# The running sum of a depthwise convolution moved from SBUF to a PSUM bank of its own

## The chip, the cores and the metric

One Trainium2 chip, one of its cores. The metric is the device time of one execution in microseconds (us); three runs of the kernel before gave 3067.32, 3067.44 and 3069.30 us, median 3067.44 us.

## The reference

Two decoder layers over 1024 tokens of width 1024, all in fp32. In each layer one projection `z = h @ w_in` feeds three things: differential attention (4 heads, two softmaxes each), a causal depthwise convolution with 31 taps over 512 channels, and the gates of the two branches.

```python
z = h @ w_in[l]                                   # q | k | v | conv input | gates
sc = where(mask, einsum('bhcqd,bhckd->bhcqk', qb, kt) * scale, neg)
p = softmax(sc); a = p[:, :, 0] - lam * p[:, :, 1]
o = rms_norm(einsum('bhqk,bhkv->bhqv', a, vt), subln_g[l])
u = ga * sigmoid(gb)
u = causal_depthwise_conv(u, dw_conv_w[l], dw_conv_b[l])      # 31 taps
y_conv = silu(layer_norm(u, conv_ln_g[l], conv_ln_b[l])) @ w_conv_o[l]
mixed = (sigmoid(gA) * (o @ w_attn_o[l]) + sigmoid(gC) * y_conv) @ w_out[l]
x = x + (1 + gate1) * mixed
x = x + (1 + gate2) * SwiGLU(rms_norm(x) * (1 + scale2) + shift2)
```

## The kernel before

Everything is held feature-major: 128 features on the partitions, 1024 tokens in two halves of 512 columns. Each fp32 operand of a matmul is split into a high and a low part, and three products (high x high, high x low, low x high) are summed in one PSUM bank, so a 128x512 output tile of the z projection is 24 matmuls. There are eight PSUM banks of 128x512 fp32, shared out to three pools: `pmain` (2 banks, `pmt`), `pscore` (3, `psct`) and `pone` (3, `p1`).

In a layer the z projection and the attention run mixed. PLAN names the order in which the parts are written: P is the projection of q, k, v of a head (tiles pq, pk, pv), A the attention of a head, g the gate projections (pg, 16 of them), C the convolution. A scheduler then fixes, before the run, the order of the instructions on each engine: it takes what is ready, by the order of writing, against a model of time. On the chip each engine runs its list strictly in order. While TensorE (PE) waits for the softmax of a block, what can stand between its attention matmuls is projection work (pk, pq, pv, pg); the text calls these the filler. There is a fixed stock of it in each layer.

The attention of a head goes in 8 blocks of 128 queries. A block has scores (psc), row maxima on VectorE (DVE), exponentials on ScalarE (ACT), the difference of the two softmaxes on DVE (L450), then for every 512 keys: up to four transposes into a bank `pat` of `pone`, a copy ath on ACT, a rest atl on DVE, and matmuls of both into a bank `po` of the same pool. po is held until DVE has read it (ov, L470). The next block needs its own po and pat. After four blocks, pot (again `pone`) turns the half head round.

The convolution comes in 8 pieces (channel group, half). Two of them run on ACT and GpSimd (POOL); the other six on DVE: one TENSOR_SCALAR for tap 0 (L607) and 30 SCALAR_TENSOR_TENSOR (L609) that read the input window `u` and the running sum `acc`, both in the SBUF tile uc, and write `acc`. That makes 180 instructions of L609 in a layer. They stand between the attention's DVE instructions wherever the scheduler saw DVE free.

At the start of layer 1, eight tiles pg of the projection (four slabs, two halves) grow together, a matmul each as the parts of h come. They use all eight banks.

Of the kernel before, what the change touches and what calls it, by code (L numbers as in the profile page):

```python
# [9 lines left out]
F32 = mybir.dt.float32  # L10
# [3 lines left out]
ALU = mybir.AluOpType  # L14
AX = mybir.AxisListType
PSUM = bass.MemoryType.PSUM
DRAM = bass.MemoryType.DRAM

P = 128
# [4 lines left out]
HF = 512  # L24
# [3 lines left out]
CONV_K = 31  # L28

CONV = ((0, 0, 0), (0, 1, 1), (1, 0, 0), (2, 0, 0), (3, 0, 0), (1, 1, 1), (2, 1, 0), (3, 1, 0))  # L30
SCB = 3
# [5 lines left out]
VB_CB = VB_CW + NCH * CONV_K  # L37
# [24 lines left out]
def trunk(tc, a):  # L62
    nc = tc.nc
    V, G, S, PE, DQ = nc.vector, nc.gpsimd, nc.scalar, nc.tensor, nc.sync
    top = ExitStack()
# [9 lines left out]
    dr = top.enter_context(tc.tile_pool(name="scratch", bufs=1, space=DRAM))  # L75
    pm = top.enter_context(tc.tile_pool(name="pmain", bufs=2, space=PSUM))
    psc = top.enter_context(tc.tile_pool(name="pscore", bufs=SCB, space=PSUM))
    p1p = top.enter_context(tc.tile_pool(name="pone", bufs=8 - 2 - SCB, space=PSUM))

    def p1(name, w=HF):  # L80
        return p1p.tile([P, w], F32, tag="p1", name=name)
# [1 line left out]
    def nt(name, w=HF, dt=F32):  # L83
        return ntp.tile([P, w], dt, tag="nt", name=name, bufs=4)

    def pmt(name):
        return pm.tile([P, HF], F32, tag="pm", name=name)

    def psct(name):
        return psc.tile([P, HF], F32, tag="sc", name=name, bufs=SCB)  # L90
# [31 lines left out]
    def vcol(l, base, j=0):  # L122
        o = l * VW + base + j
        return vec[:, o:o + 1]
# [4 lines left out]
    def wslab(src, nk, pl=None, nj=1):  # L129
        w = nk * nj * P  # L130
        raw = wp.tile([P, w], F32, tag="wraw", name="wraw", bufs=2)
        if nj > 1:
            DQ.dma_start(raw.rearrange("p (j k) -> p j k", j=nj), src.rearrange("j p k -> p j k"))
        else:
            DQ.dma_start(raw, src)
        wh, wl = ((pl or wp).tile([P, w], F32R, tag=n, name=n, bufs=2) for n in ("wh", "wl"))
        S.copy(wh, raw)  # L137
        G.tensor_tensor(wl, raw, wh.bitcast(F32), op=ALU.subtract)  # L138
        return wh, wl
# [150 lines left out]
    def sum_sq(Sq, xs, hf, j, E=None):  # L290

        hs = slice(hf * HF, hf * HF + HF)
        if j == 0:
            S.activation(Sq, xs[j][:, hs], AF.Square)
        else:
            t = nt("sqt")
            S.activation(t, xs[j][:, hs], AF.Square)
            (E or V).tensor_tensor(Sq, Sq, t, op=ALU.add)
# [17 lines left out]
    def rstd_bcast(Sq, inv_n, eps, name):  # L316

        return rstd_spread(rstd_diag(Sq, inv_n, eps, p1("pst"), 4, nt("dg")), p1(name), 4)
# [217 lines left out]
    for l in range(L):  # L536
# [27 lines left out]
        for hf in range(2):  # L564
            hs = slice(hf * HF, hf * HF + HF)
            for i in range(4):
                c = i // 2
# [19 lines left out]
        def conv(work):  # L587
            E = V
            for c, hf, on_pool in work:
                uc = cvp.tile([P, 2 * HF + CONV_K - 1], F32, tag="cv", name="uc", bufs=2)  # L590
                u, acc = uc[:, 0:HF + CONV_K - 1], uc[:, HF + CONV_K - 1:]
                if hf == 0:
                    G.memset(u[:, 0:CONV_K - 1], 0.0)
                    DQ.dma_start(u[:, CONV_K - 1:], ud[c][:, 0:HF])
                else:
                    DQ.dma_start(u, ud[c][:, HF - CONV_K + 1:T])
                for k in range(CONV_K):
                    w = vcol(l, VB_CW, c * CONV_K + k)
                    if on_pool:
                        if k == 0:  # L600
                            S.activation(acc, u[:, 0:HF], AF.Identity, bias=vcol(l, VB_CB, c), scale=w)
                        else:
                            t = A.tile([P, HF], F32, tag="ct", name="ct", bufs=1)
                            S.activation(t, u[:, k:k + HF], AF.Copy, scale=w)  # L604
                            G.tensor_tensor(acc, acc, t, op=ALU.add)  # L605
                    elif k == 0:
                        E.tensor_scalar(acc, u[:, 0:HF], w, vcol(l, VB_CB, c), op0=ALU.mult, op1=ALU.add)  # L607
                    else:
                        E.scalar_tensor_tensor(acc, u[:, k:k + HF], w, acc, op0=ALU.mult, op1=ALU.add)  # L609
                DQ.dma_start(cd[c][:, hf * HF:hf * HF + HF], acc)  # L610

        def conv_norm_steps():
# [183 lines left out]
        for hf in range(2):  # L796
            hs = HS[hf]
            Sq = nt("Sq")
            for j in range(KT):
                ps = psct("pwo")  # L800
                linear_half(ps, wslab(a["w_out"][l, j], KT), mrhs, KT, hf)
                if hf == 0:
                    DQ.dma_start(xs[j], xsrc[j])
                V.scalar_tensor_tensor(xs[j][:, hs], ps, gcol[l][0][:, j:j + 1], xs[j][:, hs],
                                       op0=ALU.mult, op1=ALU.add)
# [10 lines left out]
        for jj in range(4):  # L816
            a11, a12 = (xs[jj][:, h] for h in HS)
            a21, a22 = (xs[4 + jj][:, h] for h in HS)
            E = (V, G)[jj % 2]
# [107 lines left out]
                self.out(1, self.u4, self.c22)  # L927

        wtags = itertools.cycle(("wh", "wl"))
        banks = itertools.cycle((psct, p1, psct, p1, psct, p1, pmt, pmt))  # L930
        gs = [Group(f) for f in range(FT)]
        for g in gs[:2]:
            g.load()
# [22 lines left out]
        def gblock(hf, b):  # L956
            if b == NB - 1:
                u = hunit("gt", GP, "G", 9)
                un = [u[:, 0:2, :], u[:, 2:4, :]]
            else:  # L960
                un = [hunit(f"g{n}") if b >= 3 + hf else hunit(f"g{n}", GP, "G", 9) for n in "hl"]
            for k in range(4 * b, min(4 * b + 4, FT)):
                t = GP.tile([P, HF], F32, tag="gs", name="gs", bufs=5)
                DQ.dma_start(t, gf[k][:, HS[hf]])
                split_into(un[0][:, k % 4, :], un[1][:, k % 4, :], t, V if k % 2 else G)
            return un
# [9 lines left out]
        def ada_next(t):  # L976

            m2 = small("m2", 2)
            for h in range(2):
                raw = GP.tile([P, HF], F32, tag="gs", name="adraw", bufs=5)  # L980
                DQ.dma_start(raw, a["ada_w"][l + 1, t][:, HS[h]])
                V.scalar_tensor_tensor(raw, raw, 1.0, cs1[:, HS[h]], op0=ALU.mult, op1=ALU.mult,
                                       accum_out=m2[:, h:h + 1])
            m = modb[l + 1][:, t:t + 1]
            V.scalar_tensor_tensor(m, m2[:, 0:1], m2[:, 1:2], vcol(l + 1, t), op0=ALU.add, op1=ALU.add)
            ada_use(l + 1, t)
# [5 lines left out]
        for hf in range(2):  # L992
            hs = HS[hf]
            Sq = nt("Sq")
            for jq in range(2):
                js = range(4 * jq, 4 * jq + 4)
                pss = [(psct, psct, psct, pmt, pmt, p1, p1, p1)[j]("pfo") for j in js]
                last = hf and jq
                steps = [(b, q) for b in range(NB) for q in range(2)]
                if last:  # L1000
                    steps = [(b, q) for q in range(2) for b in reversed(range(NB))]
                seen = [0, 0]
                for b, q in steps:
                    k0, k1 = 4 * b, min(4 * b + 4, FT)
                    wh, wl = wslab(a["w_ffn_out"][l, js[2 * q]:js[2 * q] + 2, :, k0 * P:k1 * P], k1 - k0, nj=2)
                    bh, bl = gb[hf][b]
                    for jj in range(2):
                        ps = pss[2 * q + jj]
                        for k in range(k0, k1):
                            wc = slice((jj * (k1 - k0) + k - k0) * P, (jj * (k1 - k0) + k - k0 + 1) * P)  # L1010
                            PE.matmul(ps, wh[:, wc], bh[:, k % 4, :], start=(not seen[q] and k == k0), stop=False)  # L1011
                            PE.matmul(ps, wh[:, wc], bl[:, k % 4, :], start=False, stop=False)  # L1012
                            PE.matmul(ps, wl[:, wc], bh[:, k % 4, :], start=False,  # L1013
                                      stop=(seen[q] == NB - 1 and k == k1 - 1))
                    seen[q] += 1
                    for t in itertools.islice(ada_t, 3):
                        ada_next(t)
                    if hf == 0 and q == 1 and (b == 0 if jq == 0 else b < NB - 1):
                        gb[1].append(gblock(1, len(gb[1])))
                    if seen[q] == NB:  # L1020
                        for j in js[2 * q:2 * q + 2]:
                            V.scalar_tensor_tensor(xs[j][:, hs], pss[j % 4], g2[:, j:j + 1], xs[j][:, hs],  # L1022
                                                   op0=ALU.mult, op1=ALU.add)
                            sum_sq(Sq, xs, hf, j)
                            if l + 1 < L:
                                DQ.dma_start(xd[j][:, hs], xs[j][:, hs])
            pb = rstd_bcast(Sq, 1.0 / D, 1e-6, "prn")
            if l + 1 < L:
                hs_parts[hf] = norm_half(xs, hf, pb, acol[l + 1][0], modb[l + 1][:, 0:8], "h")
            else:  # L1030
                for j in range(KT):
                    y = nt("y")
                    V.scalar_tensor_tensor(y, xs[j][:, hs], vec[:, FG + j:FG + j + 1], pb,  # L1033
                                           op0=ALU.mult, op1=ALU.mult)
                    DQ.dma_start(a["out"][j][:, hs], y)
# [59 lines left out]
```

## Time and profile before

| | |
|---|---|
| median of 3 runs | 3067.44 us |
| the profiled execution | 3075.94 us, span 3074.0 us |
| busy: PE, DVE, POOL, ACT | 2800.3, 1980.2, 1779.4, 1154.6 us |
| mean granted TensorE clock | 0.964 of full speed |
| where L609 stands | 127 to 470 us (layer 1), about 1630 to 1945 us (layer 2) |

The profiled execution took 8.5 us more than the median. A row of instructions gives their busy time and the mean of one; a row of windows gives, for a stretch, how long each engine was busy in it. What PE was not busy in a stretch is what it waited there. [...]

### The profile page before, as it was taken

What the parts mean: (1) busy time and instruction counts of PE and PEld (TensorE: products, weight loads), DVE (VectorE), ACT (ScalarE), POOL (GpSimd) and SP (SyncE); (2) the same over time, 40 slices, a digit from 0 to 9 for tenths busy, and PEclk for the clock granted to TensorE, in tenths of its full rate; (3) what the DMA queues carried; (4) which work ended last, traced back from release to release, by engine and by line L of the source; (5) the groups of instructions that cost most, each with busy time, mean ns of one, the idle gap of its engine ahead of it and who ended that gap; (6) DMA issues with size and microseconds to landing.
All of it is one profiled execution on the core that took longest, in us unless ns stands there. A gap on an engine that the chain in (4) does not pass through costs nothing. (4 is left out here: it accounts for less than half of the span.)

```text
span 3074.0 us, 35430 instructions
## 1 busy us (share of the span) xinstructions
PE 2800.3 (91%) x12544; PEld 2285.4 (74%) x12544; DVE 1980.2 (64%) x2997; ACT 1154.6 (38%) x2059; POOL 1779.4 (58%) x1256
## 2 busy tenths in 40 slices
PE   4888889999979999889899888999998899998998
PEld 3666668887758888667788676788876688886786
DVE  8899997654565445578628999764546656664222
ACT  4235545443433333332322455544535233333321
POOL 6856674444676666554542686554356766666643
PEclk9989999999989999999999999999998899999999
DMA  7611111245322222388432111122552322225433
GB/s 271 223 56 66 56 59 52 83 154 203 123 103 90 83 83 83 106 264 288 155 116 89 45 53 58 66 76 84 177 192 76 123 79 84 85 83 174 138 117 93
DMA packets 151952, 353.92 MB, mean 115 GB/s; under 512 B 15328, under 2 KB 28000, under 8 KB 151776
## 3 DMA queue, kind: packets, MB, share of 16 engines
q1 hardware_dynamic: 151776, 351.67, 33.7%
q8 instruction: 99, 1.62, 0.2%
q14 instruction: 77, 0.63, 0.1%
HBM read 282.30 MB, written 69.30 MB: 114 GB/s over the span
## 5 line engine op out<-in xcount | busy, mean ns | idle before, releaser
L138 POOL TENSOR_TENSOR wl<-wraw,wh 128x1024 fp32r<-128x1024 f32 (+1 forms) x216 | 520.5, 2411 | 550.5 <-ACT wh L137 371.2
L609 DVE SCALAR_TENSOR_TENSOR uc<-uc,vec 128x512 f32<-128x512 f32 x360 | 386.7, 1074 | 5.8
L137 ACT CAST wh<-wraw 128x1024 fp32r<-128x1024 f32 (+1 forms) x216 | 219.5, 1017 | 433.3 <-PE pfo L1012 178.2
L778 POOL TENSOR_TENSOR wt<-wraw,wt 128x512 fp32r<-128x512 f32 x172 | 243.9, 1419 | 167.9 <-ACT wt L777 167.6
L1011 PE MATMUL pfo<-gh,wh 128*128 128x512 f32 x640 | 256.1, 402 | 31.1 <-ACT gh L777 22.0
L147 PE MATMUL pg<-hl,wh 128*128 128x512 f32 x640 | 253.7, 398 | 14.2 <-DVE hl L532 14.1
L146 PE MATMUL pg<-hh,wh 128*128 128x512 f32 x640 | 255.0, 403 | 11.8 <-ACT hh L531 8.9
L1013 PE MATMUL pfo<-gh,wl 128*128 128x512 f32 x640 | 243.4, 400 | 12.5 <-POOL wl L138 12.3
L1012 PE MATMUL pfo<-gl,wh 128*128 128x512 f32 x640 | 254.3, 397 | 0.0
L777 ACT CAST wt<-wraw 128x512 fp32r<-128x512 f32 x172 | 107.0, 622 | 322.7 <-PE pf L877 219.8
L605 POOL TENSOR_TENSOR uc<-uc,ct 128x512 f32<-128x512 f32 x120 | 163.6, 1363 | 66.2 <-ACT ct L604 65.4
L150 PE MATMUL pg<-hh,wl 128*128 128x512 f32 x640 | 172.6, 398 | 0.0
L439 ACT ACTIVATE e<-psc,nb 128x512 f32<-128x512 f32 (+2 forms) x192 | 110.1, 577 | 158.7 <-DVE nb L436 149.7
L1011 PEld LDWEIGHTS pfo<-gh,wh 128*128 128x128 f32 x640 | 123.8, 194 | 60.7 <-ACT gh L777 22.9
L1013 PEld LDWEIGHTS pfo<-gh,wl 128*128 128x128 f32 x640 | 123.0, 192 | 47.2 <-POOL wl L138 21.7
L147 PEld LDWEIGHTS pg<-hl,wh 128*128 128x128 f32 x640 | 121.5, 190 | 40.5 <-DVE hl L532 17.3
L1022 DVE SCALAR_TENSOR_TENSOR x<-pfo,gcol,x 128x512 f32<-128x512 f32 x32 | 23.7, 745 | 197.2 <-PE pfo L1013 196.7
L146 PEld LDWEIGHTS pg<-hh,wh 128*128 128x128 f32 x640 | 122.8, 192 | 36.3 <-ACT hh L531 9.4
L1012 PEld LDWEIGHTS pfo<-gl,wh 128*128 128x128 f32 x640 | 123.1, 192 | 25.9
L150 PEld LDWEIGHTS pg<-hh,wl 128*128 128x128 f32 x640 | 118.8, 190 | 23.4
L778 POOL TENSOR_TENSOR wt<-fraw,wt 128x512 fp32r<-128x512 f32 x88 | 118.7, 1349 | 21.1 <-ACT wt L777 21.1
L604 ACT ACTIVATE ct<-uc,vec 128x512 f32<-128x512 f32 x120 | 86.7, 722 | 113.9 <-POOL uc L605 113.0
(323 smaller groups left out, 7738.8 us busy)
## 6 DMA issues: line engine op xcount, KB each, us to landing
wraw<-in_w_ffn_out_dram SPq DMA_DIRECT2D x80, 512.0 KB
wraw<-in_w_in_dram SPq DMA_DIRECT2D x72, 512.0 KB
adraw<-in_ada_w_dram SPq DMA_DIRECT2D x48, 512.0 KB
adraw<-in_ada_w_dram SPq DMA_DIRECT2D x96, 256.0 KB
fraw<-in_w_ffn_in_dram SPq DMA_DIRECT2D x44, 512.0 KB
wraw<-in_w_ffn_in_dram SPq DMA_DIRECT2D x44, 512.0 KB
gs<-gf SPq DMA_DIRECT2D x88, 256.0 KB
gd<-graw SPq DMA_DIRECT2D x64, 256.0 KB
```

The source lines that it names most:

```text
L137: S.copy(wh, raw)
L138: G.tensor_tensor(wl, raw, wh.bitcast(F32), op=ALU.subtract)
L146: PE.matmul(ps, wh[:, wc], rhs(0, k, hf), start=(k == 0), stop=False)
L147: PE.matmul(ps, wh[:, wc], rhs(1, k, hf), start=False, stop=False)
L150: PE.matmul(ps, wl[:, wc], rhs(0, k, hf), start=False, stop=(k == nk - 1))
L439: S.activation(e[:, n0:n1], pss[b][:, 0:n1 - n0], AF.Exp, bias=nb, scale=0.125, accum_out=sx[:, 2 * b + c:2 * b + c + 1])
L605: G.tensor_tensor(acc, acc, t, op=ALU.add)
L609: E.scalar_tensor_tensor(acc, u[:, k:k + HF], w, acc, op0=ALU.mult, op1=ALU.add)
L778: E.tensor_tensor(lo, src, hi.bitcast(F32), op=ALU.subtract)
L1011: PE.matmul(ps, wh[:, wc], bh[:, k % 4, :], start=(not seen[q] and k == k0), stop=False)
L1012: PE.matmul(ps, wh[:, wc], bl[:, k % 4, :], start=False, stop=False)
L1013: PE.matmul(ps, wl[:, wc], bh[:, k % 4, :], start=False, stop=(seen[q] == NB - 1 and k == k1 - 1))
```

## The change

A fourth PSUM pool, `pconv`, has one bank (`pct`); `pone` has two banks instead of three. On DVE, taps 0 to 29 now write the running sum to that bank and read it from there; tap 30 reads it there and writes `acc` in SBUF, from where the transfer to DRAM goes as before. The two pieces on ACT and POOL are as they were. Two lists of banks in the feed-forward part take the new bank in the place of the third of `pone`.

```diff
-    p1p = top.enter_context(tc.tile_pool(name="pone", bufs=8 - 2 - SCB, space=PSUM))
+    p1p = top.enter_context(tc.tile_pool(name="pone", bufs=8 - 3 - SCB, space=PSUM))
+    pcv = top.enter_context(tc.tile_pool(name="pconv", bufs=1, space=PSUM))
...
+    def pct(name):
+        return pcv.tile([P, HF], F32, tag="pc", name=name)
...
                     elif k == 0:
-                        E.tensor_scalar(acc, u[:, 0:HF], w, vcol(l, VB_CB, c), op0=ALU.mult, op1=ALU.add)
+                        pc = pct("pc")
+                        E.tensor_scalar(pc, u[:, 0:HF], w, vcol(l, VB_CB, c), op0=ALU.mult, op1=ALU.add)
                     else:
-                        E.scalar_tensor_tensor(acc, u[:, k:k + HF], w, acc, op0=ALU.mult, op1=ALU.add)
+                        E.scalar_tensor_tensor(pc if k + 1 < CONV_K else acc, u[:, k:k + HF], w, pc,
+                                               op0=ALU.mult, op1=ALU.add)
...
-        banks = itertools.cycle((psct, p1, psct, p1, psct, p1, pmt, pmt))
+        banks = itertools.cycle((psct, p1, psct, p1, psct, pct, pmt, pmt))
...
-                pss = [(psct, psct, psct, pmt, pmt, p1, p1, p1)[j]("pfo") for j in js]
+                pss = [(psct, psct, psct, pmt, pmt, p1, p1, pct)[j]("pfo") for j in js]
```

Since the scheduler sees other pools, the order moves too. Three places follow. Line numbers of the changed kernel are higher by 4 above the convolution and by 6 below it.

First DVE in layer 1, at the end of the second convolution piece, before:

```order
L609 SCALAR_TENSOR_TENSOR uc_3416<-uc_3416,vec_104 128x512
L436 TENSOR_SCALAR nb_1506<-mx_1500 128x1
L436 TENSOR_SCALAR nb_1516<-mx_1510 128x1
L446 RECIPROCAL r_1474<-sx_1453 128x2
L448 TENSOR_SCALAR f_1476<-sx_1453,r_1474,nlam_128 128x1
L450 SCALAR_TENSOR_TENSOR e_1462<-e_1472,f_1476,e_1462 128x256
L461 TENSOR_TENSOR atl_1440<-pat_1437,ath_1439 128x128
```

And the same place now:

```order
L614 SCALAR_TENSOR_TENSOR uc_3420<-uc_3420,vec_107,pc_3423 128x512
L454 SCALAR_TENSOR_TENSOR e_1422<-e_1432,f_1436,e_1422 128x128
L438 TENSOR_REDUCE mx_1467<-psc_1468 128x1
L440 TENSOR_SCALAR nb_1473<-mx_1467 128x1
L438 TENSOR_REDUCE mx_1503<-psc_1504 128x1
L450 RECIPROCAL r_1477<-sx_1456 128x2
```

The sum now comes from pc, and the piece ends earlier as counted in attention work: its last tap stood behind the first block's difference (L450, 128x128) and now stands ahead of it. Over a layer, the last tap on DVE stood ahead of the 17th of the 32 blocks' normalization in layer 1 and of the 16th in layer 2; now it stands ahead of the 16th and the 14th.

Second PE in layer 1, from the last attention matmuls to the first one of the branch product (py), before; pg is filler, oh the split attention output:

```order
L147 MATMUL pg_5706<-hl1_239,wh_5674 128x512
L479 MATMUL pot_5208<-ident_100,o4_4905 128x128
L146 MATMUL pg_5706<-hh1_237,wh_5674 128x512
...
L150 MATMUL pg_5706<-hh0_236,wl_5675 128x512 x4
L150 MATMUL pg_5706<-hh1_237,wl_5675 128x512 x4
L146 MATMUL py_5823<-oh_5738,wh_5819 128x512
```

And the same place now, from the last block's transposes:

```order
L461 MATMUL pat_5175<-ident_103,e_5150 128x128 x4
L469 MATMUL po_5174<-vs_4446,ath_5180 128x256
L471 MATMUL po_5174<-vs_4446,atl_5181 128x128
...
L461 MATMUL pat_5192<-ident_103,e_5150 128x128 x4
L469 MATMUL po_5174<-vs_4446,ath_5197 128x256
L471 MATMUL po_5174<-vs_4446,atl_5198 128x128
...
L483 MATMUL pot_5217<-ident_103,o4_4914 128x128 x4
L150 MATMUL py_5832<-oh_5747,wh_5828 128x512
```

The filler that stood among the last blocks has moved ahead of them: behind the last pg there are now 112 attention matmuls and nothing else (18 psc, 60 po, 26 pat, 8 pot: the products of the fifth-last block, and transposes, products and most scores of the last four). In layer 2, too, the last pg stands ahead of the products of the fifth-last block.

Third PE near the start of layer 1, where the eighth pg began among the others, before:

```order
L146 MATMUL pg_662<-hh0_236,wh_276 128x512
L146 MATMUL pg_716<-hh0_236,wh_326 128x512
L147 MATMUL pg_716<-hl0_238,wh_326 128x512
L147 MATMUL pg_635<-hl0_238,wh_251 128x512
L146 MATMUL pg_635<-hh0_236,wh_251 128x512
```

And where it stands now:

```order
L154 MATMUL pg_692<-hh0_239,wl_305 128x512 x4
L154 MATMUL pg_692<-hh1_240,wl_305 128x512 x4
L150 MATMUL pg_719<-hh0_239,wh_329 128x512
L151 MATMUL pg_719<-hl0_241,wh_329 128x512
L150 MATMUL pg_719<-hh0_239,wh_329 128x512
```

With seven banks at hand the eighth tile starts when the other seven are complete.

## Rows read from the trace of the kernel before

**Rows 1.** The page's first part: busy us, share of the span, instructions.
```profile
PE 2800.3 (91%) x12544; PEld 2285.4 (74%) x12544; DVE 1980.2 (64%) x2997; ACT 1154.6 (38%) x2059; POOL 1779.4 (58%) x1256
```

**Rows 2.** Windows: stretch, length, busy (count) of PE, PEld, DVE, ACT, POOL, clock, DMA.
```profile
127.00:470.00 343.00, 296.90 (x1362) 235.59 (x1360) 325.28 (x494) 152.81 (x311) 222.27 (x169) 0.96 0.21 74
470.00:650.00 180.00, 174.53 (x928) 149.79 (x929) 106.21 (x265) 86.02 (x212) 82.05 (x89) 0.98 0.22 74
1630.00:1700.00 70.00, 68.07 (x294) 55.87 (x293) 58.76 (x69) 13.72 (x18) 22.07 (x14) 0.98 0.25 87
1700.00:1945.00 245.00, 211.70 (x981) 168.59 (x980) 234.34 (x361) 123.18 (x266) 173.63 (x127) 0.94 0.15 52
1945.00:2115.00 170.00, 166.37 (x886) 142.51 (x885) 107.48 (x266) 81.50 (x208) 77.77 (x83) 0.99 0.22 74
```

**Rows 3.** L609: all (shortest/median/longest ns), then 127:470 and 1630:1945 (busy, mean).
```profile
L609 DVE SCALAR_TENSOR_TENSOR uc<-uc,vec x360: 726/753/2977, 127.0 to 1939.9; 128x512 f32<-128x512 f32 x180
...
L609 DVE SCALAR_TENSOR_TENSOR uc<-uc,vec 128x512 f32<-128x512 f32 x180 | 194.9, 1083 | 2.4
...
L609 DVE SCALAR_TENSOR_TENSOR uc<-uc,vec 128x512 f32<-128x512 f32 x171 | 185.0, 1082 | 3.1
```

**Rows 4.** Timeline, 306 to 313 us, DVE and POOL: start, length, engine.
```profile
307.53 2.97 DVE L609 SCALAR_TENSOR_TENSOR uc<-uc,vec 128x512 f32<-128x512 f32 x1
307.55 2.41 POOL L138 TENSOR_TENSOR wl<-wraw,wh 128x1024 fp32r<-128x1024 f32 x1
...
311.13 0.67 DVE L361 TENSOR_TENSOR t<-pq,Ct 128x512 f32<-128x512 f32 x1
311.31 1.28 POOL L362 TENSOR_TENSOR t<-t,St 128x512 f32<-128x512 f32 x1 [1.35 <-DVE t L360]
```

**Rows 5.** One line with PSUM and SBUF inputs, same operation and size: L804.
```profile
L804 DVE SCALAR_TENSOR_TENSOR x<-pwo,gcol,x x32: 736/751/753, 746.8 to 2338.9; 128x512 f32<-128x512 f32 x32
```

**Rows 6.** Who PE waited for, 127 to 470 us: total, times, longest.
```profile
PE psc L430 <- ACT e L439: 11.3, 11, 2.8
...
PE pat L457 <- DVE ov L470: 1.8, 1, 1.8
```

**Rows 7.** Timeline of PE, 106 to 129 us: the wait after the first projection tiles.
```profile
120.11 3.78 PE L150 MATMUL pgb<-hh,wl 128*128 128x512 f32 x8 [13.37 <-POOL wl L138]
...
127.62 1.98 PE L150 MATMUL pgb<-hh,wl 128*128 128x512 f32 x8
```

**Rows 8.** Timeline, 625 to 649 us: one block's chain at attention's end.
```profile
625.00 0.60 PE L457 MATMUL pat<-ident,e 128*128 128x128 f32 x4
625.36 0.93 PE L150 MATMUL pg<-hh,wl 128*128 128x512 f32 x3
625.64 0.59 ACT L460 CAST ath<-pat 128x512 fp32r<-128x512 f32 x1 [0.49 <-PE pat L457]
...
626.26 0.69 DVE L461 TENSOR_TENSOR atl<-pat,ath 128x512 fp32r<-128x512 f32 x1 [4.70 <-ACT ath L460]
...
637.52 0.33 PE L465 MATMUL po<-vs,ath 128*128 128x256 f32 x1
...
637.75 0.34 PE L465 MATMUL po<-vs,ath 128*128 128x256 f32 x1
...
638.48 0.42 DVE L470 TENSOR_REDUCE ov<-po 128x128 f32<-128x256 f32 x1 [5.16 <-PE po L467]
...
639.77 0.55 POOL L475 TENSOR_TENSOR ss<-ss,nhalf 128x1 f32<-128x1 f32 x1 [10.95 <-DVE ss L474]
...
642.66 0.45 POOL L476 TENSOR_SCALAR o<-ov,r,ss 128x128 f32<-128x128 f32 x1
...
645.76 3.89 ACT L693 CAST oh<-oT 128x1024 fp32r<-128x1024 f32 x4
```

**Rows 9.** DVE by line, 470 to 650 us: count, busy, mean ns.
```profile
L434 DVE TENSOR_REDUCE mx<-psc 128x1 f32<-128x512 f32 (+3 forms) x44 | 24.4, 567 | 7.2 <-PE psc L433 6.5 <-PE psc L431 0.5
L450 DVE SCALAR_TENSOR_TENSOR e<-e,f 128x384 f32<-128x384 f32 (+7 forms) x14 | 14.9, 1063 | 0.4
```

## The prediction

> **What bounds the kernel now.** I read the page's busy times first: PE is busy for 91% of the span, so a change can only pay where PE is not [rows 1]. Then the windows around the convolution. While L609 is at work DVE is nearly never free (325.3 of 343 us in layer 1, 234.3 of 245 in the second part of layer 2), and PE is idle for 46.1 and 33.3 us; once the convolution is over, DVE falls to 59% and PE waits 5.5 of 180 us [rows 2]. So in two stretches of some 600 us together DVE sets the pace, and the rest belongs to PE. The clock adds to it: a wait of 13.37 us is followed by eight matmuls at 3.78 us instead of 1.98 [rows 7], and the mean clock is 0.96 and 0.94 in those stretches [rows 2]. [...]
>
> Over the five windows PE's idle time is 46.1+5.5+1.9+33.3+3.6 = 90.4 us, the clock's loss 13.7+3.6+1.4+14.7+1.7 = 35.1 us: 125.5 us is the most that the change can win. PE's own need in the 1008 us is 882.5 us.
>
> **Why L609 is slow.** Its shortest is 0.726 us and its median 0.753, but the mean is 1.08 [rows 3]. One that started 0.02 us before a POOL subtraction of 2.41 us took 2.97 us; right after, a DVE instruction with one input in PSUM took 0.67 us beside a POOL multiplication [rows 4]. Same operation and size with one input in PSUM: 32 times 736 to 753 ns, none stretched [rows 5]. So two inputs in SBUF collide with POOL, one does not.
>
> **The change, part by part.**
>
> The taps: I take 0.75 us for one that reads the sum from PSUM [rows 5]. That frees 180 x (1.083-0.75) = 60 us of DVE in layer 1's stretch and 171 x (1.082-0.75) = 57 us in 1630 to 1945 us [rows 3]. No row shows DVE writing to PSUM. Bounds: 0.73 us (the shortest today) and 1.08 (today's mean, no gain); I take the PSUM reader's value, the nearest row.
> [...]
>
> DVE's need in 127 to 470 us becomes 325.3-60 = 265 us; PE's is 343-46.1-13.7 = 283. In 1630 to 1945 us it becomes 293.1-57 = 236 against PE's 315-35.2-16.1 = 264 [rows 2]. DVE is no longer the longer one: PE is late next. Its waits then should look like those of 470 to 650 us, where DVE is not full: 5.5 idle and 3.6 by clock, 9.1 us on a need of 170.9 [rows 2].
>
> The tap 0 instruction (12 of them), the transfer of `acc` and POOL's pieces: nothing on the path. The feed-forward lists still go round eight banks. In the branch products a `pone` bank comes round every eighth tile instead of every twelfth, as `pmain`'s does already. All at zero.
>
> The eighth pg at the start: 16 matmuls move behind the others, 16 x 0.25 = 4 us (1.98 us for eight). Behind them PE waits 13.37 us for a weight split on POOL [rows 7], which hides them. Without that cover it costs 4 us.
>
> The lost bank of attention: the scheduler answered by giving every block more filler, so that the stock runs out before the last four blocks of each layer. In the kernel before, this place costs PE nothing, since pg stands there. Now it is a bare chain. A round of four transposes takes 1.95 us from the first transpose to the end of atl, then four pairs of po at 0.23 us: 2.9 us [rows 8]. Two banks (one po, one pat) let no round overlap the next. Five rounds are of four tiles, 14.5 us; those of 1, 2 and 3 tiles I put at 1.0, 1.5 and 2.1 us, in proportion. With the 0.9 us of the fifth-last block's po that is 20 us. At the end come ov, square, power and scaling (638.48 to 640.32 and 0.45), the last pot and oT (1.1, four transposes and one pass of DVE out of PSUM [rows 5]), the cast oh (a quarter of 3.89) and 0.3 for the handovers: 4.7 us [rows 8]. Sum 24.7 us. In the same DVE queue stand 4 differences (4.3 us) and some 14 maxima (7.9) of these blocks [rows 9]. The differences lie on the way to the next transposes, so I count them whole, and of the maxima half: 33 us. Bounds: 24.7 if all of them hide, 36.9 if none does. PE's own work in it is 30 pairs of po (6.9), 34 transposes (3.1, four start within 0.36 us [rows 8]) and 18 scores at no more than 0.25 (4.5): 14.5 us. Loss 18.5 us a layer, bounds 10.2 and 22.4. PE then starts again at the lower clock, 1.8 us as in [rows 7].
>
> The sum: outside the tails PE needs 882.5-29 = 853.5 us and loses 9.1/170.9 of it, 45.4 us. The tails lose 2 x (18.5+1.8) = 40.6. Together 86 instead of 125.5: a gain of 39.5 us. The profiled execution would go from 3075.9 to 3036.4; the median stands 8.5 us lower, so 3028 us.
>
> **The rivals.**
>
> A second limit takes DVE's place, no bank at all. PE's scores wait for the exponentials that free a score bank, 11.3 us of 46, more than for anything else [rows 6]. If this chain through ACT, not DVE's load, sets the pace, two thirds of today's loss stay (84 us), and with the tails' 40.6 it comes to 124.6: no change, 3066 us. For it: that row. Against: ACT is busy for 153 of 343 us only [rows 2], so its lateness comes from DVE.
>
> Two banks bind in every block, not only in the last ones. The next block's transposes need the bank that DVE frees with ov. It shows already with three banks, but only as one wait of 1.8 us [rows 6]. 56 blocks stand outside the tails; with w us of such a wait each, the loss is 86+56w, so from w = 0.71 us the change is slower. At 1.2 us, two thirds of that longest wait, it is 153 against 125.5: 3095 us. Against it: within a head at least some 20 filler matmuls stand from one block to the next, 5 us of cover, though not always where the wait falls.
> [...]
>
> The change does not do what it says: a tap that also writes PSUM keeps today's mean of 1.08 us. Then 125.5 stays, the tails come on top: 3108 us. Against it only [rows 5], which read PSUM and do not write it.
>
> **How the numbers follow.** Forecast (faster, 3028 us) 0.66; limit through ACT (3066) 0.13; banks bind everywhere (3095) 0.14; taps no faster (3108) 0.07. The forecast's own range: pre-tail loss 27 us (5.3 of 170, as in 1945 to 2115 us) to 63 (half of today's), tails 20 to 45, clock 3.6: gains of 74 to 14 us, 2993 to 3053. The range that should hold 8 in 10 goes up into the bank rival: 2998 to 3090. What a measurement here can tell from no change is 0.2%, 6 us. Faster: 0.66 x 0.95 and 0.13 x 0.4, 0.68. Slower: 0.14+0.07 and a quarter of 0.13, 0.24. Within: the rest, 0.08.
>
> **What would show it.** The taps' row: a mean near 0.75 with no long ones; above 0.9 the first step is wrong. POOL's instructions in the two stretches should be shorter too. DVE's share in 127 to 470 us: 85 to 90%, with PE above 93%. Between the last pg and the first py of each layer: 30 to 36 us in which PE is under half busy; a tail under 20 or over 42 us means that I mis-sized it. If PE's waits show pat after ov in block after block, the bank rival holds.

## The result and the profile after

The changed kernel takes 2989.9 us (median of four runs, 2983.78 to 2992.24) against 3068.4 us for the kernel before, run beside it: a ratio of 0.9738, 95% interval 0.9723 to 0.9754. Forecast were 3028 us and a range of 2998 to 3090. The direction was right; the gain is 78 us where 39.5 were forecast, and the time lies below the range. All that follows compares the profiled executions: a span of 2988.2 us now, 3074.0 before, 85.8 us less. Some 8 us of that belong to the executions and not to the kernels: the profiled one before took 8.5 us more than its median, this one 0.2 more than its own.

The page's head and first part, columns as in [rows 1]:

```profile
span 2988.2 us, 35455 instructions
PE 2783.1 (93%) x12544; PEld 2284.7 (76%) x12544; DVE 1836.9 (61%) x2997; ACT 1158.0 (39%) x2059; POOL 1719.9 (58%) x1256
```

DVE has 143 us less to do than in [rows 1] (117 of them at the taps, 360 x (1.074 - 0.750) by the means on the two pages), POOL 59 us less, and PE loses only 17 us of its busy time; so the gain is waiting that went, not work. The taps, counterpart of [rows 3] (shortest/median/longest ns):

```profile
L614 DVE SCALAR_TENSOR_TENSOR pc<-uc,vec,pc x348: 730/755/759, 125.2 to 1832.9; 128x512 f32<-128x512 f32 x174
L612 DVE TENSOR_SCALAR pc<-uc,vec x12: 804/814/816, 124.3 to 1791.7; 128x512 f32<-128x512 f32 x12
```

The median stands where it stood (755 ns, 753 before), and the long ones are gone: the longest is 759 ns where it was 2977. The mean, 750 ns, is the 0.75 us of the forecast. POOL's conv additions show the other half of the collision; first the kernel before, then the changed one, from the page's fifth part:

```profile
L605 POOL TENSOR_TENSOR uc<-uc,ct 128x512 f32<-128x512 f32 x120 | 163.6, 1363 | 66.2 <-ACT ct L604 65.4
```

```profile
L609 POOL TENSOR_TENSOR uc<-uc,ct 128x512 f32<-128x512 f32 x120 | 139.0, 1158 | 57.5 <-ACT ct L608 56.8
```

And a few moments of both engines side by side, from the timeline of the changed kernel, to be held against [rows 4]: a tap that starts while POOL adds takes 0.76 us, three in a row beside another addition 2.33 us, and that addition 1.09 us.

```profile
332.74 1.53 POOL L609 TENSOR_TENSOR uc<-uc,ct 128x512 f32<-128x512 f32 x1
...
334.03 0.76 DVE L614 SCALAR_TENSOR_TENSOR pc<-uc,vec,pc 128x512 f32<-128x512 f32 x1
...
336.68 2.33 DVE L614 SCALAR_TENSOR_TENSOR pc<-uc,vec,pc 128x512 f32<-128x512 f32 x3
...
337.36 1.09 POOL L609 TENSOR_TENSOR uc<-uc,ct 128x512 f32<-128x512 f32 x1
```

Now the windows (columns as in [rows 2]): for each layer the stretch with the taps, the stretch behind them up to the last pg, and the bare tail up to the first py; layer 2 has one more at its start.

```profile
127.00:399.00 272.00, 263.09 (x1255) 218.04 (x1254) 257.88 (x465) 143.11 (x288) 188.64 (x163) 0.97 0.25 87
399.00:574.50 175.50, 172.88 (x909) 146.92 (x908) 101.16 (x248) 77.62 (x193) 82.09 (x83) 1.00 0.24 82
574.50:611.20 36.70, 25.85 (x114) 19.84 (x112) 19.19 (x42) 14.18 (x41) 8.01 (x11) 0.68 0.30 108
1560.00:1630.00 70.00, 70.00 (x314) 58.10 (x313) 56.11 (x81) 15.62 (x21) 14.56 (x11) 1.00 0.24 79
1630.00:1856.00 226.00, 223.53 (x1106) 186.74 (x1105) 206.70 (x379) 131.16 (x271) 164.01 (x140) 1.00 0.21 72
1856.00:2038.10 182.10, 182.10 (x961) 155.56 (x960) 94.82 (x252) 82.46 (x202) 85.16 (x86) 1.00 0.24 84
2038.10:2071.40 33.30, 22.66 (x113) 17.57 (x112) 16.81 (x39) 13.69 (x38) 7.93 (x11) 0.76 0.34 119
```

Read them as the prediction read those of before: idle time plus (1-c) of the stretch, c being the mean clock. The clock records of both traces hold 1.00 and 0.50 only, so 2(1-c) of a stretch stood at 0.50. There eight matmuls took 3.58 us from the first start to the start behind them, and 1.82 at 1.00 (120.11 and 127.62 us in the kernel before): half the rate, so (1-c) is the estimate of what the clock takes. The two tails lose 10.9 + 11.7 and 10.6 + 8.0 us, 41.2 in all. The five other stretches lose 8.9 + 8.2, 2.6, 0, 2.5 and 0: 22 us. Both layers gain alike: the first py starts at 611.2 us instead of 650.6 and at 2071.4 instead of 2155.5, 39.4 us and then 44.7 more.

Who PE still waited for from 127 to 400 us (total, times, longest), to be held against [rows 6]:

```profile
PE pgb L154 <- POOL wl L142: 4.7, 1, 4.7
PE pq L150 <- DVE t L365: 2.0, 1, 2.0
PE po L469 <- DVE atl L465: 0.8, 1, 0.8
...
PE psc L434 <- ACT e L443: 0.6, 2, 0.4
PE pat L461 <- DVE oT L484: 0.2, 1, 0.2
```

The waits for exponentials fell from 11.3 us to 0.6 with no change to ACT, and no pat waits for ov here. The bare tail of layer 1, from the timeline of PE:

```profile
572.66 2.01 PE L154 MATMUL pg<-hh,wl 128*128 128x512 f32 x8
...
577.84 0.66 PE L461 MATMUL pat<-ident,e 128*128 128x128 f32 x4 [1.03 <-DVE ov L474]
580.79 0.33 PE L483 MATMUL pot<-ident,o 128*128 128x128 f32 x1 [2.29 <-POOL o L480]
...
592.81 1.07 PE L461 MATMUL pat<-ident,e 128*128 128x128 f32 x4
594.62 0.58 PE L469 MATMUL po<-vs,ath 128*128 128x256 f32 x1 [0.73 <-ACT ath L464]
```

The last pg is followed by bare chains: transposes, a wait for ath, products, the next transposes. Four transposes that took 0.60 us in [rows 8] take 1.07 at 592.81, for the granted clock is 0.68 over this stretch and 0.50 from 592.7 us to its end: among the waits the work between them is slow too.

### The profile page after: what moved, and what is told of

Its sections match the earlier page's. It is cut to its first block, busy times and chain, and to the rows that moved or that the text cites. A ratio compares the mean times of both kernels' runs of the same rounds, so it can differ in the third digit from the quotient of the medians.

```text
span 2988.2 us, 35455 instructions
## 1 busy us (share of the span) xinstructions
PE 2783.1 (93%) x12544; PEld 2284.7 (76%) x12544; DVE 1836.9 (61%) x2997; ACT 1158.0 (39%) x2059; POOL 1719.9 (58%) x1256
## 5 line engine op out<-in xcount | busy, mean ns | idle before, releaser
L142 POOL TENSOR_TENSOR wl<-wraw,wh 128x1024 fp32r<-128x1024 f32 (+1 forms) x216 | 513.0, 2376 | 587.1 <-ACT wh L141 391.2
L614 DVE SCALAR_TENSOR_TENSOR pc<-uc,vec,pc 128x512 f32<-128x512 f32 x348 | 261.1, 750 | 6.0
L609 POOL TENSOR_TENSOR uc<-uc,ct 128x512 f32<-128x512 f32 x120 | 139.0, 1158 | 57.5 <-ACT ct L608 56.8
L438 DVE TENSOR_REDUCE mx<-psc 128x1 f32<-128x512 f32 (+2 forms) x192 | 102.7, 549 | 23.8 <-PE psc L437 16.0
```

Source lines behind the costliest of these rows:

```text
L614: E.scalar_tensor_tensor(pc if k + 1 < CONV_K else acc, u[:, k:k + HF], w, pc, op0=ALU.mult, op1=ALU.add)
```

## The experiments

Times are medians. The kernel before took 3068.4 us beside the changed kernel, 3068.65 us beside the first four kernels and 3073.7 us beside the other four; ratios are to it, and a difference in us between the changed kernel and one of the last four carries these 5 us.

**The bank alone.** The changed kernel with its four pools and its lists, but the taps keep their sum in SBUF, so that the banks that attention has are those of the changed kernel and the taps' operands differ. The order is near that of the changed kernel, not the same: in layer 1 the same 112 attention matmuls stand behind the last pg, in layer 2 only 66.

```diff
-                        E.scalar_tensor_tensor(pc if k + 1 < CONV_K else acc, u[:, k:k + HF], w, pc,
+                        E.scalar_tensor_tensor(acc, u[:, k:k + HF], w, acc,
```

> The pools of the changed kernel (two banks for attention, the fourth pool's bank idle in attention), but all taps keep their sum in SBUF as in the kernel before. The order stays close to the changed kernel's: the last four blocks of layer 1 have no filler. Theory (the taps' collision with POOL is the whole gain, the bank costs two bare tails of about 20 us): taps at 1.05 to 1.10 us, PE idle again 40 to 50 us in layer 1's convolution, tails on top: 3095 to 3115 us. Rival (the gain comes from the new order with more filler between blocks, the taps matter little): 2985 to 3020 us. Second rival (bank and order cost nothing where DVE paces): 3060 to 3075 us.

Measured: 3100.3 us, ratio 1.0096 (1.0076 to 1.0117). The page's row of the taps, and a window of the stretch with them:

```profile
L613 DVE SCALAR_TENSOR_TENSOR uc<-uc,vec 128x512 f32<-128x512 f32 x360 | 387.8, 1077 | 6.0
```

```profile
150.00:450.00 300.00, 259.07 (x1165) 205.64 (x1165) 287.04 (x412) 135.98 (x279) 193.99 (x142) 0.95 0.17 59
```

The time is in the theory's range, and PE is idle for 40.9 of these 300 us, as the theory had it. The two halves of the change part here. Taking the bank away costs 31.6 us (3100.3 - 3068.65), moving the sum into it brings 110.4 us (3100.3 - 2989.9); how much the difference of order adds to either number was not tried. The taps shrink by 360 x (1.077-0.750) = 118 us: the time fell by nearly as much as DVE got free.

**The sum in one of attention's three banks.** The kernel before, three banks in `pone`, and the sum takes its bank from there.

```diff
-                        E.tensor_scalar(acc, u[:, 0:HF], w, ...)
+                        pc = p1("pc")
+                        E.tensor_scalar(pc, u[:, 0:HF], w, ...)
```

> No fourth pool: DVE's running sum takes a bank of attention's own pool of three, so attention has two while a piece runs and three after it. Filler lasts to the end of each layer's attention again. Theory (taps cheap, the tails are the price of the lost bank): taps at 0.75 us, no bare tail, 2990 minus two tails of 15 to 20 us: 2950 to 2962 us. Rival (two banks during the convolution are what costs, the tail only shows it; the convolution now reaches to the 25th block): 2980 to 3000 us.

Measured: 3211.8 us, ratio 1.0461 (1.0446 to 1.0477), beyond both expectations. The taps take 750 ns here too; the loss is in the waits of PE, here those of layer 1 (layer 2 has a wait of 69.4 us of the same kind):

```profile
PE pat L457 <- DVE uc L610: 69.3, 1, 69.3
PE po L465 <- ACT ath L460: 33.6, 3, 32.4
```

The banks of a pool are handed out in turn. A transpose got the bank that a conv piece was still summing in, and PE stood for 69 us until the piece's last tap; the clock was 0.53 from 400 to 500 us. A sum that holds its bank for some 45 us (six pieces in 275 us in the changed kernel) and transposes that are read within 2 us [rows 8] do not go together in one pool; that the sum has a pool of its own matters more than the third bank (222 us between this kernel and the changed one, 31.6 for the bank).

**The taps long again, without a collision.** The changed kernel with a maximum over 256 columns of the sum's bank behind each tap, 0.42 us each, which reads PSUM only.

```diff
+                        E.reduce_max(pad, pc[:, 0:PADW], axis=AX.X)
```

> The changed kernel with one more DVE instruction for each tap, a maximum over 256 columns of the sum's PSUM bank (0.41 us by the row of 128x256 maxima, about 0.33 start to start), its result unused: DVE carries as much per tap as before, with no collision and known to the scheduler, which spreads the convolution to the 25th block. Theory A (DVE's load itself was the limit): 3040 to 3070 us. Theory B (what hurt was load the order did not know of, behind which PE's list waited): PE below 3% idle in the convolution and filler to the end, 2960 to 3005 us.

Measured: 3102.1 us, ratio 1.0104 (1.0083 to 1.0126); the time is in the range of neither. The windows say why, first the taps' stretch, then the 150 us behind it, and the largest wait of PE in the second:

```profile
150.00:400.00 250.00, 246.75 (x1226) 205.78 (x1226) 239.84 (x502) 137.05 (x289) 159.07 (x137) 1.00 0.21 70
400.00:550.00 150.00, 86.91 (x349) 68.20 (x348) 113.34 (x244) 39.33 (x101) 38.00 (x45) 0.65 0.09 30
```

```profile
PE pmu L641 <- DVE csum L635: 42.7, 2, 39.6
```

DVE is 96% full from 150 to 400 us, as full as in the first experiment (287.04 of 300), and PE is at 99% there instead of 86%. A full DVE by itself did not hold PE back here. The order knew of the maxima and put the taps further apart: the last stood ahead of the 25th block's normalization instead of the 16th's. The price came later. In layer 1 the convolution's norm waited for the sum, 42.7 of the 63.1 us that PE is idle in the second stretch, and the clock fell to 0.65. In layer 2 that wait is 7.5 us only, and the loss stands where the last taps leave attention with little filler:

```profile
1930.00:2040.00 110.00, 78.77 (x322) 61.38 (x322) 91.78 (x219) 35.69 (x106) 20.59 (x30) 0.67 0.12 39
```

In the first experiment the order has the taps about where those of 0.75 us stand (the last one ahead of the 16th block in layer 1 and the 15th in layer 2; the 16th and the 14th in the changed kernel), and on the chip they take 1.08: the attention's DVE instructions behind them in the queue are late, and PE with them. That it is this lateness fits both runs; it was not tried alone.

**Two banks for the scores, three for attention.** The changed kernel with `SCB = 2`.

```diff
-SCB = 3
+SCB = 2
```

> The sum's bank is taken from the scores' pool (two instead of three), attention's transposes keep three; one list of banks in the feed-forward part takes a bank of the latter pool for the third of the former. Filler lasts to the last block in layer 1 and the second-last in layer 2. Theory (the bare tail is the price of the bank in the changed kernel): 2950 to 2970 us. Rival (scores wait for the exponentials, the longest wait of PE before, so two banks cost more there): 2990 to 3040 us.

Measured: 2975.6 us, ratio 0.969 (0.9674 to 0.9707): some 14 us faster than the changed kernel, but 6 us above the expected range. The bank is better missed at the scores than at the transposes. From 127 to 600 us PE waited most for exponentials, 5.3 us; in the changed kernel it was 3.3 us in the same stretch, so at most 2 us of the price moved there.

**The sum's bank lent to the transposes.** Once the convolution is over, every second pat of the third and fourth head takes it.

```diff
+        patb = itertools.cycle((p1, pct) if late else (p1,))
...
-                    pt = p1("pat")
+                    pt = next(patb)("pat")
...
-                attend_head(l, A, qkv.pop(n), oT[n])
+                attend_head(l, A, qkv.pop(n), oT[n], n >= 2)
```

> The changed kernel, with one difference: from the third head of a layer on (the convolution's last tap stands ahead of the 16th block, so the sum's bank is free), every second bank of transposes (pat) comes from the sum's bank. The filler then lasts to the end of attention in both layers, so there is no bare tail. Theory (the two bare tails cost 41 us, 22.6 and 18.6, and they come from the missing bank alone): 2950 to 2968 us, and PE over 45 of 50 us busy in every stretch up to the first py. Rival (the tails are only where a loss shows that the chain of transposes would cost anyway, spread over the blocks): 2980 to 2995 us.

Measured: 2937.7 us (2936.1 to 2939.0), ratio 0.9559 (0.9545 to 0.9573), the fastest kernel here, 52 us below the changed one and 12 below the expected range. Its stretch behind the taps up to the first py, then the first py of layers 1 and 2:

```profile
399.00:578.60 179.60, 178.92 (x980) 153.57 (x981) 119.31 (x289) 89.37 (x227) 88.03 (x93) 1.00 0.22 76
```

```profile
L150 PE MATMUL py<-oh,wh x64: 389/389/389, 578.6 to 647.9; 128*128 128x512 f32 x64
...
L150 PE MATMUL py<-oh,wh x64: 389/389/389, 2016.3 to 2085.7; 128*128 128x512 f32 x64
```

PE is never idle for long and the clock stays at 1.00: the bare tail is gone. Layer 1 reaches py 32.6 us earlier than in the changed kernel, layer 2 another 22.5; at each of these points some 5 us are work that only moved, since 24 matmuls of pg now stand behind the first py of either layer. With the bank lent the tails are gone, so they came from the missing bank, as the prediction said, and cost at least the 41 us read from the windows. Where the other 11 us came from I can only estimate: the tails' matmuls at full rate, by the distances between starts, are 11.6 and 11.3 us, which leaves 25.1 and 22.0 us of loss where busy time and clock showed 22.6 and 18.6; and from 127 to 399 us the clock was 0.99 instead of 0.97, 5 us.

**Both.** Two score banks, and from the third head on every third score goes to the sum's bank.

```diff
+        scb = itertools.cycle((psct, psct, pct) if late else (psct,))
...
-                        ps = psct("psc")
+                        ps = next(scb)("psc")
```

> The kernel with two banks for scores and three for transposes and products, which took 2975.6 us; from the third head on every third score goes to the sum's bank, so that scores have three banks again where the convolution is over. Theory (the price of two score banks is paid in the second half of a layer, where PE waited for exponentials): 2955 to 2970 us. Rival (what is left there is the last blocks' own chain, whichever bank is added): 2972 to 2980 us.

Measured: 2959.2 us, ratio 0.963 (0.9616 to 0.9645), in the theory's range, and 16 us less than with two score banks alone. The theory's reason is not borne out: from 127 to 600 us PE still waits 4.0 us for exponentials (5.3 without the loan), and layer 1 reaches its first py only 1.5 us earlier (595.8 us, 597.3 without). Where the rest came from stays open. Lent to the transposes of the changed kernel, the same bank is worth 52.

**Fewer taps, sum in PSUM.** The changed kernel without taps 16 to 29 in DVE's pieces.

```diff
+                    if not on_pool and 16 <= k < CONV_K - 1:
+                        continue
```

> The changed kernel with 14 of the 31 taps (16 to 29) of DVE's six pieces left out in each layer: 168 instructions less, 126 us of DVE. Theory (after the change DVE's load costs PE no more than about 10 of the 22 us that PE was not at full work ahead of the tails, and the filler now lasts longer, so that some 30 of the 41 us of the tails go): 2945 to 2968 us. Rival (the convolution still holds PE back in waits too short for the busy times to show): 2920 to 2944 us.

Measured: 2963.1 us, ratio 0.9642 (0.9625 to 0.9658): 27 us less than the changed kernel for 126 us less on DVE, in the theory's range. The order has filler into the last block of layer 2 here and runs out three blocks before the end in layer 1 (24 and 66 attention matmuls stand behind the last pg, 112 in each layer of the changed kernel), so a good part of the 27 is a tail that went. DVE's load no longer sets the pace: nearly half of the taps' time off DVE brings a fifth of it.

**Fewer taps, sum in SBUF.** The same 14 taps left out of the kernel before.

> The kernel before with the same 14 taps (16 to 29) of DVE's six pieces left out, sum in SBUF, three banks, no bare tail. It measures what the convolution's load costs in the kernel before. Theory (freed of it, PE loses what it lost from 500 to 650 us, some 1 to 2 per cent, and the busy times of PE hid some 20 us more): 2950 to 2975 us. The prediction's reading (PE keeps losing 45 us of its 125 by the share read from 470 to 650 us, nothing hidden): 2980 to 3000 us.

Measured: 2994.1 us, ratio 0.9745 (0.973 to 0.9759). The theory that I held by then missed, and the time lies in the range that I had given to the prediction's reading. The windows do not bear that reading out, though. First 100 us amid the taps, then the stretch behind the last one (358.8 us):

```profile
150.00:250.00 100.00, 84.57 (x370) 67.25 (x370) 90.54 (x117) 37.93 (x69) 54.87 (x40) 0.95 0.21 71
360.00:600.00 240.00, 239.58 (x1274) 204.71 (x1274) 151.29 (x348) 120.98 (x293) 132.16 (x127) 1.00 0.22 74
```

While the remaining 96 taps of the layer run (mean 1.06 us), PE loses as much as before: 15 us idle in 100 (46.1 in 343 in [rows 2]). Behind them it loses 0.4 of 240 us. What I had overlooked is that leaving taps out shortens the bad stretch and does not mend what remains of it. Fewer taps free 182 us of DVE (168 x 1.083) and bring 80 us; shorter taps freed 118 and brought 110.

## Why the prediction was right or wrong

**The taps: right.** 0.75 us was forecast, 750 ns is the mean, and none is stretched. The first experiment shows that no more than the operands is needed for it (1077 ns a tap with the sum in SBUF and the same banks), and the rival "taps no faster" falls. The medians, 755 ns with the sum in PSUM and 753 within SBUF, lie 2 ns apart. Beside POOL a tap with both inputs in SBUF took 2.97 us [rows 4], one with the sum in PSUM 0.76 (the four timeline lines above). The prediction's own words, that two inputs in SBUF collide with POOL and one does not, are too wide: tap 0 of the kernel before has one input tensor in SBUF, and some of the twelve are stretched, up to 1858 ns.

```profile
L607 DVE TENSOR_SCALAR uc<-uc,vec x12: 534/625/1858, 126.2 to 1878.7; 128x512 f32<-128x512 f32 x12
```

**The bare tails: right in place and length, in their price partly by luck.** 30 to 36 us each were forecast, 36.7 and 33.3 are there, and they lose 41.2 us against 40.6. The parts are others, though: 18.5 us of waiting and 1.8 of clock were forecast for each, and 10.9 and 10.6 of waiting, 11.7 and 8.0 of clock are read. PE is busy for 70 and 68% of them and not under half, because its work there runs largely at the lower clock (0.68 and 0.76 over the two stretches). Lending the bank takes the tails away. The price of the bank is not one number, however: 31.6 us with slow taps (first experiment), at least 41 with fast ones, 52 by what lending it brings.

**The eighth pg: right.** PE still waits for the same weight and takes eight matmuls at the lower clock behind it (3.78 us, 0.50 from 116 to 120 us); the wait is 5.87 us where it was 13.37 in [rows 7], and the taps begin 1.8 us earlier than before.

```profile
116.08 3.78 PE L154 MATMUL pgb<-hh,wl 128*128 128x512 f32 x8 [5.87 <-POOL wl L142]
```

**What PE loses outside the tails: the step that failed.** The prediction put it so: "PE is late next. Its waits then should look like those of 470 to 650 us, where DVE is not full: 5.5 idle and 3.6 by clock, 9.1 us on a need of 170.9". That share, carried over 853.5 us, gave 45.4 us; 22 are measured by the same reading. The mechanism was right, DVE handed the pace to PE, and the term was sized twice too large; that is 23 of the 46 us by which the profiled gain, 85.8 us, passed the forecast. The window was not a clean sample of the term. The kernel before, with that window and its counterpart in layer 2 cut where the wake of the last taps ends:

```profile
470.00:500.00 30.00, 26.27 (x128) 22.46 (x129) 19.85 (x56) 14.51 (x40) 11.30 (x14) 0.89 0.17 62
500.00:650.00 150.00, 148.26 (x802) 127.33 (x801) 86.36 (x210) 71.51 (x172) 70.75 (x75) 1.00 0.22 76
1945.00:1975.00 30.00, 27.16 (x145) 23.13 (x144) 22.30 (x55) 15.49 (x39) 10.79 (x13) 0.94 0.25 85
1975.00:2155.00 180.00, 178.79 (x944) 152.84 (x943) 97.52 (x238) 81.09 (x198) 85.18 (x88) 1.00 0.23 80
```

The first 30 us hold 3.7 us of idle time and a clock of 0.89; the other 150 lose 1.2%, in layer 2 0.7%. One per cent of 853.5 us would have been 9 us, a gain of 76 and about 2992 us; the measured 22 lies between the two. The last experiment and the one with the lent bank show the clean share again: 0.2% and 0.4% behind the taps. The prediction's own lower end, 27 us from 1945 to 2115 us, had the same wake in it, which is why the range stopped at 2993 for this case and at 2998 in all.

**What remains.** Losses read from the windows fall from 125.5 to 63.4 us, 62 of the 85.8: 55 us of idle time and 7 of clock. The other 24 us lie in what that reading leaves out. The trace shows a matmul as busy for 0.39 us though the next starts 0.23 later, so a wait below 0.16 us between two leaves no idle time. A count by the distances between starts, each against that of an undisturbed pair, shows such waits too. From the first pg to the first py it covers 610.4 and 563.8 us of the two layers before, 570.9 and 521.5 now: 81.8 us less. The matmuls' own time is the same within 2 us, so nothing was saved in matmuls. Idle time fell by 60 us (118.4 to 58.3), the lower clock costs 12 to 14 us less, and the waits too short to show fell by some 10, an estimate that moves by a microsecond or so with what is called undisturbed. So of the 24 us about 5 are idle time ahead of the taps, 5 to 7 clock, 10 short waits, and 4 lie outside the two stretches. Idle time plus (1-c) misjudges the clock because it counts a slow clock as lost also where PE waits anyhow, which is much of the tails. No run shows by itself the 35.1 us of clock in the prediction's sum; the runs show half the rate at 0.50, and a clock that by the starts costs 12 to 14 us less where (1-c) fell by 7. And 125.5 us is not the most that can be won in these stages: the kernel with the lent bank is 136 us faster than the kernel before (3073.7 - 2937.7).

**The rivals.** The limit through ACT falls: its waits went with DVE's load. The bank rival falls too, for PE waits for no ov before the tail: the one gap of [rows 6] does not come back from block to block. It was near in another form, though: with the bank shared in one pool, a single wait of 69 us in each layer did more than all the banks of 56 blocks.

## What to carry to other kernels

Before a share of lost time is carried from one window to another, cut the window at the end of whatever you mean to remove: the wake of a late stretch reaches past its last instruction. An engine that is 95% full says little by that alone: it held PE to 86% where its instructions ran longer than their place in the order allowed (first experiment), and the same fullness, planned, left PE at 99% where it stood (third experiment; that the lateness is the reason fits, and is not shown by itself). Count waits by the distances between starts, and not by idle time alone. And a bank taken for one stage can be lent back when the stage is over: that was worth two thirds as much again as the change itself.

## What the runs showed of the hardware

A multiply-add of 128x512 fp32 on DVE with input and output in PSUM took what one within SBUF took, 755 against 753 ns, but the tap 0 TENSOR_SCALAR did not: 814 ns into PSUM (above), and 548 ns at the median within SBUF in the last experiment; at that price 12 of them make 3 us, which the prediction put at zero. Within SBUF it was held up, though it has one input tensor: five of the twelve in the kernel before took 1.09 to 1.86 us, and each ended 0.28 or 0.29 us after a POOL instruction that had begun before it. Into PSUM all twelve took 804 to 816 ns, also those that began beside a POOL instruction. The maximum over 256 columns out of PSUM took 419 ns. DVE's records stand in the order of its list where that is printed: the changed kernel's last tap of the second piece starts at 209.79 us, and e, mx, nb, mx and r follow from 210.45 to 212.07 us as listed ahead of the prediction.
